# Seven block products in place of eight for 15 of 22 gate and up pairs of each feed-forward stage

## The chip, the cores and the metric

The kernel runs on one core of a Trainium2 chip. The metric is the time of one execution on the device in microseconds (us), as the median of several runs. The profile comes from one execution more, which a hardware profiler recorded.

The engines are TensorE (PE in the profile, with its weight loads apart as PEld), VectorE (DVE), ScalarE (ACT), GpSimd (POOL) and SyncE (SP). SBUF is the memory on the chip, PSUM the accumulators that TensorE writes; a PSUM tile here is one bank, 128 partitions by 512 numbers of 32 bits.

## The reference

Two layers of an encoder over 512 tokens of width 1024, all in float32. Each layer has three stages: feed-forward 1, a mixer (three kinds of attention, gates, a projection), feed-forward 2. Only the feed-forward stages change:

```python
def swiglu(x, w_gu, w_down):
    gate, up = jnp.split(x @ w_gu, 2, axis=-1)
    return (jax.nn.silu(gate) * up) @ w_down
...
y = swiglu(rmsnorm(h, ffn1_pre_g[l]), ffn1_w_gu[l], ffn1_w_down[l])
h = h + 0.5 * rmsnorm(y, ffn1_post_g[l])
```

Here `w_gu` is 1024 x 5632 (2816 gate columns, then 2816 up columns) and `w_down` 2816 x 1024. `rmsnorm` divides each token by the root of the mean of its squares plus 1e-6 and multiplies by a gain.

## The kernel before

**Layout.** Activations lie transposed: a tile is 128 of the 1024 channels on the partitions by 512 tokens. `h` is eight such tiles (KD = 8). The weights come as blocks of 128 x 128 in the order in which the program uses them (the list `order`), eight blocks (512 KB) to a DMA, `wr`, of which three buffers exist.

**Three products for one.** Every number is taken apart into a rounded part hi (type fp32r) and the rest lo, and a block product is three matmuls, hi x hi, hi x lo, lo x hi (`mm3`, L235 to L237), all summed in PSUM. The weights are taken apart on the fly by `ensure`: for each half of a `wr` tile, four blocks or 128 x 512, one ACT copy makes `wh` (L193) and one DVE subtraction makes `wl` (L194). `wblk` (L198) calls `ensure` two half tiles ahead of the use and issues the fetches, on the ACT queue. There are four buffers each of `wh` and `wl`.

**A feed-forward stage** (`ffn`, L413). The operand X is `h` times the gain of the pre-norm, in hi and lo; it is not divided by the root yet, since that scale (`rB`, one number for each token, the same on all partitions) is known only when the squares are summed. `begin` (L314) does the first three block columns in two halves of 256 tokens, as the stage before it ends. Then for each of KF = 22 pairs m a gate column block and an up column block are formed, 8 x 3 matmuls of 512 columns each, into PSUM tiles tagged mm and at. `finish` (L423) takes a pair: DVE gate times rB (L425), ACT Silu (L426), DVE times up (L427), then the split into hi and lo (L258 on ACT, L259 on DVE); up is not scaled by rB, which the norm behind the down projection takes out (its small constant is corrected by `e2`). Then `end` (L338) does the down projection, seven of eight row blocks whole, the last in two halves (`part`), while `refresh` updates `h` and makes the next operand.

**What sets the order.** The program is written in one stream; a scheduler places each engine's instructions from it, and buffers and semaphores do the rest. TensorE's stream of a pair is 24 matmuls into mm, then 24 into at. A tile of a pool that is used again waits until its last reader is done; a wait on a PSUM tile is for the whole tile.

Of the kernel before, what the change touches and what calls it, by code (L numbers as in the profile page):

```python
# [32 lines left out]
PAD = {"f": 168, "m": 168}  # L33
# [77 lines left out]
def encoder_kernel(ctx: ExitStack, tc: tile.TileContext, order, xT, wts, cols, rows, rpb, consts, tables, out):  # L111
# [9 lines left out]
    BUFS = {"h": 8, "x": 24, "t": 6, "r": 2, "wr": 3, "wh": 4, "wl": 4}  # L121
    ABUFS = {"f": {"a": 2 * KF}, "m": {"rr": 3, "tx": 5, "st": 16, "g": 10, "s": 2, "pt": 4}}
# [33 lines left out]
    rowt = cp.tile([P, L, ROWW], F32, tag="rowt", name="rowt")  # L156
    ones = cp.tile([P, P], F32, tag="ones", name="ones")
    half = cp.tile([P, NCOLS], F32, tag="half", name="half")
    misc = cp.tile([P, 2 * L + 1], F32, tag="misc", name="misc")
# [12 lines left out]
    stream = {"raw": [], "ready": [], "made": 0, "held": {}, "limit": 0}  # L172
# [9 lines left out]
    def ensure(n):  # L182
        while stream["made"] < min(n, NTILES * 2):
# [4 lines left out]
            if i in stream["held"]:  # L188
                tag = stream["held"][i]
                hi, lo = (big(tag, F32R, (P, HB, P), name="w") for _ in range(2))  # L190
            else:
                hi, lo = (sb.tile([P, HB, P], F32R, tag=t, name=nm(t), bufs=BUFS[t]) for t in ("wh", "wl"))
# [39 lines left out]
    V.tensor_scalar(out=half, in0=colt, scalar1=0.5, scalar2=None, op0=ALU.mult)  # L232

# [41 lines left out]
    def inv_rms(squares, n, nt, extra=None):  # L275
# [4 lines left out]
        if extra is None:  # L280
            V.tensor_scalar(out=ms[:, :nt], in0=tot[:, :nt], scalar1=1.0 / n, scalar2=EPS, op0=ALU.mult, op1=ALU.add)
        else:
            V.scalar_tensor_tensor(
                out=ms[:, :nt], in0=tot[:, :nt], scalar=1.0 / n, in1=extra, op0=ALU.mult, op1=ALU.add
            )
        A.activation(r[:, :nt], ms[:, :nt], AF.Sqrt)
        V.reciprocal(out=r[:, :nt], in_=r[:, :nt])
        rep = spread(r, nt)
        return rep, ms
# [24 lines left out]
    def begin(refresh, X, first, spare):  # L314
# [5 lines left out]
        stream["held"] = {i: spare for i in range(at + BUFS["wh"], stream["limit"])}  # L320
# [8 lines left out]
    def finish_rms(s):  # L329
        rB = big("r", name="rB")  # L330
        rep, ms = inv_rms(s.acc, D, NT)
        V.tensor_copy(rB, rep)
        return rB, rep, ms

    def fresh():
        return [(big("x", F32R, name="hi"), big("x", F32R, name="lo")) for _ in range(KD)]

    def end(name, l, X, group, tail, gcol, e2, after, hold=()):  # L338

        y = [big("x", name="y") for _ in range(KD)]  # L340
# [6 lines left out]
        if hold:  # L347
            at = len(order) + (KD - tail) * len(X)
            assert at % HB == 0 and len(hold) * HB == tail * len(X)
            stream["held"] = {at // HB + i: tag for i, tag in enumerate(hold)}  # L350
# [9 lines left out]
        def scales(i):  # L360
            hs = HALVES[i]
            extra = e2[:, 2 * i : 2 * i + 2] if e2 is not None else None
            return inv_rms(s.acc[:, hs], D, 2, extra)[0]
# [48 lines left out]

    def ffn(l, which, refresh, X):  # L413
        gu, dn = f"ffn{which}_w_gu", f"ffn{which}_w_down"
        firsts = [(gu, l, 0, 0), (gu, l, 0, KF), (gu, l, 0, 1)]
        (g0, u0, g1), s = begin(refresh, X, firsts, "a")
        u1 = dense1(gu, l, KF + 1, X, tag="at")
        rB, _, ms = finish_rms(s)
        e2 = small("e2", NT, 2)
        V.tensor_scalar(out=e2, in0=ms, scalar1=EPS, scalar2=None, op0=ALU.mult)  # L420
        act = []

        def finish(pg, pu):  # L423
            t = big("t", name="t")
            V.tensor_tensor(out=t, in0=pg, in1=rB, op=ALU.mult)  # L425
            A.activation(t, t, AF.Silu)  # L426
            V.tensor_tensor(out=t, in0=t, in1=pu, op=ALU.mult)  # L427
            act.append(split(t, "a"))

        finish(g0, u0)  # L430
        finish(g1, u1)
# [341 lines left out]
    for l in range(L):  # L773
        with open_phase("f"):
            refresh, X = ffn(l, 1, refresh, X)
        if l == 0:
            prepare()
# [62 lines left out]
```

## Time and profile before

| | |
|---|---|
| median of 3 runs | 2534.66 us (2534.31 to 2537.56) |
| the profiled execution | 2534.24 us, of which the span of the profile is 2532.5 |
| granted TensorE clock | 0.998 of full speed |
| matmuls | 12274 |
| read from HBM | 231.16 MB, 94 GB/s over the span |

The span is from the first to the last recorded instruction. In a row of a group of instructions come the line, the engine, the operation, the tile written and the tiles read (buffer numbers left out), the shape, the count, then the busy time, the mean of one in ns, and behind the second bar the idle time of the engine just before them with what ended most of it. A matmul's recorded duration is longer than its share of the stream, since matmuls overlap in the array: what one costs is the distance from its start to the next start.

### The profile page before, as it was taken

The page shows a single profiled execution, that of the slowest core. Times are in us where ns is not written, and L with a number is a line of the kernel's source. Part 1 is how long each engine was busy: PE and PEld are TensorE (multiplying, and loading weights), DVE is VectorE, ACT ScalarE, POOL GpSimd, SP SyncE. Part 2 cuts the span into 40 slices and gives each one's busy share as a digit, 9 for nine tenths or more (in the row PEclk, how much of TensorE's full clock was granted, in tenths as well). Part 3 has the DMA queues.
Part 4 walks back from the last instruction along what each step waited for, and adds up shares of the span by engine and source line. Part 5 has one row for each costly group of instructions (what it writes and reads, how often), then busy time and mean ns, then how long its engine had stood idle before and what let it go on. Part 6 is the DMA issues. An engine that isn't in the chain of part 4 may idle for free.

```text
span 2532.5 us, 32765 instructions
## 1 busy us (share of the span) xinstructions
PE 2506.4 (99%) x12274; PEld 2103.0 (83%) x12274; DVE 1380.1 (54%) x2687; ACT 1116.3 (44%) x2163; POOL 215.6 (9%) x197
## 2 busy tenths in 40 slices
PE   9999999999999999999999999999999999999998
PEld 8888888888778888888888888888887788888887
DVE  5444248867776464442364442488687764644423
ACT  5333245646555453333343332456465554533322
POOL 0000011001111220000110000200001112100002
PEclk9999999999999999999999999999999999999999
DMA  4232237435443322222232223374344423232222
GB/s 157 94 100 94 98 99 218 119 109 138 114 125 99 108 76 93 99 100 92 92 100 100 92 100 100 112 211 113 108 131 130 116 95 105 75 100 95 97 100 83
DMA packets 97375, 277.87 MB, mean 110 GB/s; under 512 B 13504, under 2 KB 17984, under 8 KB 97216
## 3 DMA queue, kind: packets, MB, share of 16 engines
q10 hardware_dynamic: 59616, 216.63, 25.9%
q1 hardware_dynamic: 37600, 59.15, 9.2%
q8 instruction: 96, 1.57, 0.3%
q14 instruction: 63, 0.52, 0.1%
HBM read 231.16 MB, written 6.29 MB: 94 GB/s over the span
## 4 chain that ended last, share of the span: by engine, by line
PE 91%; DVE 3%; issue 2%; DMA 1%; ACT 1%; POOL 1%; SPq 1%; POOLq 0%; DVEq 0%; ACTq 0%
PE mm L237 19%; PE mm L236 19%; PE mm L235 19%; PE at L236 9%; PE at L235 9%; PE at L237 9%; PE at L512 1%; POOL h L392 1%; PE o L515 1%; PE o L516 1%; PE at L484 1%; DMA sh<-raw 1%; PE at L269 1%; PE at L631 1%; PE at L485 1%
## 5 line engine op out<-in xcount | busy, mean ns | idle before, releaser
L193 ACT ACTIVATE wh<-wr 128x512 fp32r<-128x512 f32 x812 | 511.3, 631 | 1005.7 <-PE at L236 506.6
L194 DVE TENSOR_TENSOR wl<-wr,wh 128x512 fp32r<-128x512 f32 x812 | 582.7, 719 | 651.3 <-ACT wh L193 642.7
L237 PE MATMUL mm<-hi,wl 128*128 128x512 f32 (+1 forms) x2372 | 899.0, 379 | 4.8 <-DVE wl L194 4.4
L235 PE MATMUL mm<-hi,wh 128*128 128x512 f32 (+1 forms) x2372 | 897.1, 378 | 1.3 <-ACT wh L193 1.1
L236 PE MATMUL mm<-lo,wh 128*128 128x512 f32 (+1 forms) x2372 | 896.7, 378 | 0.1
L237 PEld LDWEIGHTS mm<-hi,wl 128*128 128x128 f32 x2372 | 447.2, 189 | 83.3 <-DVE wl L194 7.9
L235 PEld LDWEIGHTS mm<-hi,wh 128*128 128x128 f32 x2372 | 447.2, 189 | 77.8 <-ACT wh L193 1.3
L236 PEld LDWEIGHTS mm<-lo,wh 128*128 128x128 f32 x2372 | 447.3, 189 | 76.4 <-DVE lo L310 0.3
L235 PE MATMUL at<-hi,wh 128*128 128x512 f32 (+1 forms) x1028 | 394.3, 384 | 0.0
L236 PE MATMUL at<-lo,wh 128*128 128x512 f32 (+1 forms) x1028 | 393.8, 383 | 0.0
L237 PE MATMUL at<-hi,wl 128*128 128x512 f32 (+1 forms) x1028 | 393.6, 383 | 0.0
L235 PEld LDWEIGHTS at<-hi,wh 128*128 128x128 f32 x1028 | 193.5, 188 | 37.8
L237 PEld LDWEIGHTS at<-hi,wl 128*128 128x128 f32 x1028 | 193.5, 188 | 37.7
L236 PEld LDWEIGHTS at<-lo,wh 128*128 128x128 f32 x1028 | 193.4, 188 | 37.5
L304 POOL TENSOR_TENSOR ss<-ss,sq 128x512 f32<-128x512 f32 (+1 forms) x38 | 46.9, 1233 | 1391.3 <-ACT sq L303 1390.2
L427 DVE TENSOR_TENSOR t<-t,at 128x512 f32<-128x512 f32 x88 | 60.1, 687 | 127.4 <-PE at L237 124.2
L425 DVE TENSOR_TENSOR t<-mm,rB 128x512 f32<-128x512 f32 x88 | 60.5, 691 | 121.5 <-PE mm L237 121.3
L258 ACT ACTIVATE hi<-at 128x256 fp32r<-128x256 f32 (+2 forms) x168 | 75.8, 472 | 69.3 <-PE at L512 31.0
L259 DVE TENSOR_TENSOR lo<-at,hi 128x256 fp32r<-128x256 f32 (+2 forms) x168 | 87.1, 533 | 18.0 <-ACT hi L258 16.6
L392 POOL TENSOR_TENSOR h<-h,y 128x256 f32<-128x256 f32 x92 | 77.0, 867 | 83.2 <-DVE y L390 83.2
L530 POOL TENSOR_TENSOR sh<-sh,sinR 128x512 f32<-128x512 f32 x26 | 34.3, 1319 | 545.1 <-DMA sh<-raw 329.6
L497 ACT ACTIVATE s<-s,nmx 128x256 f32<-128x256 f32 (+1 forms) x128 | 70.4, 552 | 14.0 <-DVE nmx L488 7.5
(146 smaller groups left out, 2145.0 us busy)
## 6 DMA issues: line engine op xcount, KB each, us to landing
wr<-in_wts_dram ACTq DMA_DIRECT2D x413, 512.0 KB, 3.2
st<-hi SPq DMA_DIRECT2D x84, 128.0 KB, 2.3
st<-lo SPq DMA_DIRECT2D x84, 128.0 KB, 2.3
sh<-raw SPq DMA_DIRECT2D x104, 64.0 KB, 2.0
sw<-lo SPq DMA_DIRECT2D x36, 128.0 KB, 3.5
sw<-hi SPq DMA_DIRECT2D x36, 128.0 KB, 3.0
braw<-in_rpb_dram SPq DMA_DIRECT2D x16, 256.0 KB
kept<-h SPq DMA_DIRECT2D x16, 256.0 KB, 2.0
```

The costliest lines, as they stand in the source:

```text
L193: A.activation(hi, raw, AF.Copy)
L194: V.tensor_tensor(out=lo, in0=raw, in1=f(hi), op=ALU.subtract)
L235: PE.matmul(acc, w[0], x[0], start=start, stop=False)
L236: PE.matmul(acc, w[0], x[1], start=False, stop=False)
L237: PE.matmul(acc, w[1], x[0], start=False, stop=stop)
L258: A.activation(hi, src, AF.Copy)
L259: V.tensor_tensor(out=lo, in0=src, in1=f(hi), op=ALU.subtract)
L304: eng.tensor_tensor(out=self.acc[:, cs], in0=self.acc[:, cs], in1=sq[:, cs], op=ALU.add)
L392: adder.tensor_tensor(out=h[b][:, hs], in0=h[b][:, hs], in1=y[b][:, hs], op=ALU.add)
L425: V.tensor_tensor(out=t, in0=pg, in1=rB, op=ALU.mult)
L427: V.tensor_tensor(out=t, in0=t, in1=pu, op=ALU.mult)
L497: A.activation(ss[i], ss[i], AF.Exp, scale=-scale, bias=nmx[:, i : i + 1], accum_out=l[:, i : i + 1])
```

## The change

**Which products.** For the last 15 pairs of a stage (`PLAIN = 7` stay as they were) gate and up are no longer two separate columns of products. The pair's weights are a 2 x 2 matrix of blocks (gate, up by the first and second half of the 1024 channels) and the activation is a 2 x 2 matrix too (halves of channels by halves of tokens). Their product, eight block products in the plain way, is formed by seven, after Strassen and Winograd: `p1` to `p7`. Each is four blocks deep (HK = 4), three matmuls for each block, over 256 tokens: 84 matmuls of 256 columns for a pair (L648), where 48 of 512 stood. The operands of the products are sums and differences of the parts.

**Activation.** Since the sums of channels mix numbers of different tokens' halves, the activation is normalised first: `normal` multiplies by gain and rB (DVE, eight times). `less` makes the four differences t1 to t4, `divide` the hi and lo parts of the four parts and the differences. All that is put in a list, `stream["later"]`, of which each new weight half tile of the plain pairs runs one piece (`wblk`).

**Weights of a group.** A group is a pair done in this way. Its two `wr` tiles are fetched by the SP queue (`fetches`). DVE makes the sums `sum13` (128 x 1024), `sum2`, `sum4` (128 x 512) and the lo parts `low1`, `low13`, `low24` (128 x 1024) and `low12` (128 x 512); ACT makes the hi parts `high1`, `high13`, `high24` (128 x 1024) and `high12`.

**Accumulators.** A group has one PSUM tile mm with two halves, a and c, and half of one of two PSUM tiles at, b, which two matmuls a stage open (`seeds`). p1 goes into a; `seed` copies a to b on ACT (L688); p7 goes into c; `copy7` copies c to SBUF (L692); p6 adds to a; `copy2` copies a to SBUF (L695); p4 adds to c; `add21` on DVE adds c to that copy (L699); p2 adds to b, p5 to a; `add22` adds a (L703); p3 adds to a. At the end b and a hold the gate of the two token halves (`silu0`, `silu1`), and the SBUF tile v holds up with the sign turned; `gated` multiplies (L715).

**Behind it.** The result `act` stays in float32 and is taken apart late, by `cut` (L730, L731), during the last group and the down projection (three pieces to a weight half tile, `pace`). The sign goes into the post gain (`nhalf`, -0.5), and `e2` goes, as gate and up are both scaled now. Buffers: the 24 single x tiles become 12 pairs, `wh` and `wl` (4 each) four pairs `wp`. `prepare`, some small work on the lambdas and sinks, moves into the first feed-forward stage.

The core of the diff:

```diff
-    BUFS = {"h": 8, "x": 24, "t": 6, "r": 2, "wr": 3, "wh": 4, "wl": 4}
+    BUFS = {"h": 8, "x": 12, "t": 6, "wr": 3, "wp": 4}
...
+            for _ in range(min(stream["pace"], len(stream["later"]))):
+                stream["later"].pop(0)()
             stream["tile"] = stream["ready"].pop(0)
...
-        def finish(pg, pu):
-            t = big("t", name="t")
+        def finish(m, pg, pu):
+            t, v = big("t", name="t"), big("t", name="v")
             V.tensor_tensor(out=t, in0=pg, in1=rB, op=ALU.mult)
             A.activation(t, t, AF.Silu)
-            V.tensor_tensor(out=t, in0=t, in1=pu, op=ALU.mult)
-            act.append(split(t, "a"))
+            V.scalar_tensor_tensor(out=v, in0=pu, scalar=-1.0, in1=rB, op0=ALU.mult, op1=ALU.mult)
...
+            V.tensor_tensor(out=act[m], in0=t, in1=v, op=ALU.mult)
...
-        for m in range(2, KF):
-            finish(dense1(gu, l, m, X), dense1(gu, l, KF + m, X, tag="at"))
...
+        for m in range(2, PLAIN):
+            finish(m, dense1(gu, l, m, X), dense1(gu, l, KF + m, X, tag="at"))
...
+        def product(acc, w, x, start, stop):
+            for k in range(HK):
+                ws, xs = (w[0][:, k, :], w[1][:, k, :]), (hi[x][:, k, :], lo[x][:, k, :])
+                for n, (i, j) in enumerate(((0, 0), (0, 1), (1, 0))):
+                    PE.matmul(
+                        acc, ws[i], xs[j], start=start and k == n == 0, stop=stop and k == HK - 1 and n == 2,
+                        skip_group_check=True,
+                    )
...
+        def seed(g):
+            A.activation(groups[g]["b"], groups[g]["a"], AF.Copy)
...
+        for g in range(count):
+            more, last = g + 1 < count, g + 1 == count
+            p1(g)
+            if g:
+                add22(g - 1)
+            low24(g)
+            if more:
+                high1(g + 1)
+            seed(g)
+            if more:
+                sum13(g + 1)
+            p7(g)
+            if more:
+                high13(g + 1)
+                low1(g + 1)
+            copy7(g)
...
+            if g:
+                p3(g - 1)
+            if more:
+                sum2(g + 1)
+            if g:
+                silu1(g - 1)
+            if more:
+                high12(g + 1)
+            if g:
+                gated(g - 1)
+            p6(g)
+            if more:
+                low13(g + 1)
...
+            copy2(g)
+            p4(g)
+            add21(g)
...
+            p2(g)
+            silu0(g)
+            if more:
+                low12(g + 1)
+                sum4(g + 1)
+                fetches(g + 2)
+                p5(g)
+                high24(g + 1)
```

**TensorE, where one group's p7 begins.** The scheduler interleaves two groups. Here mm_1239 is the PSUM tile of the new group, mm_1120 that of the group before it; h_520 belongs to the last matmuls of p1, h_878 to p3 of the group before, ht_601 to p7. `[waits ...]` names the engine that is waited for.

```order
L648 MATMUL mm_1239<-h_520,h_1136 128x256
L648 MATMUL mm_1239<-l_521,h_1136 128x256
L648 MATMUL mm_1239<-h_520,l_1155 128x256
L648 MATMUL mm_1120<-h_878,h_1118 128x256 [waits DVE_49]
L648 MATMUL mm_1120<-l_879,h_1118 128x256
L648 MATMUL mm_1120<-h_878,l_1134 128x256
L648 MATMUL mm_1120<-h_878,h_1118 128x256
L648 MATMUL mm_1239<-ht_601,h_1153 128x256 [waits Activation_49]
L648 MATMUL mm_1239<-lt_602,h_1153 128x256
```

Four matmuls of p3 stand between p1's last and p7's first, which waits for the copy `seed` on ACT; p3 itself waits for `add22` on DVE. Over the whole group TensorE goes p1 (one matmul), p5 of the group before (12), p1 (11), p3 (4), p7 (12), p3 (8), p6 (12), p2 (4), p4 (12), p2 (8). In the kernel before the stream of a pair waits for weight parts alone, as where the next gate block begins:

```order
L236 MATMUL at_1282<-lo_134,wh_1266 128x512
L237 MATMUL at_1282<-hi_133,wl_1267 128x512
L235 MATMUL mm_1325<-hi_119,wh_1285 128x512 [waits Activation_49]
L236 MATMUL mm_1325<-lo_120,wh_1285 128x512
L237 MATMUL mm_1325<-hi_119,wl_1286 128x512 [waits DVE_49]
```

**DVE, one pair before and one group now.** Before, wl is a weight's lo part, the others belong to `finish`:

```order
L194 TENSOR_TENSOR wl_1598<-wr_1595,wh_1597 128x512
L425 TENSOR_TENSOR t_1629<-mm_1559,rB_432 128x512
L194 TENSOR_TENSOR wl_1614<-wr_1595,wh_1613 128x512
L194 TENSOR_TENSOR wl_1641<-wr_1638,wh_1640 128x512
L427 TENSOR_TENSOR t_1629<-t_1629,at_1594 128x512
L194 TENSOR_TENSOR wl_1657<-wr_1638,wh_1656 128x512
L259 TENSOR_TENSOR lo_1634<-t_1629,hi_1633 128x512
```

Now, from `add21` of one group to `sum13` for three groups later (add21, sum2, low12, sum4, add22, low1, low13, low24, gated, sum13):

```order
L699 TENSOR_TENSOR v_1394<-mm_1357,v_1394 128x256
L560 TENSOR_TENSOR wr_1459<-r_1494,wr_1457 128x512
L567 TENSOR_TENSOR w_1528<-wr_1459,w_1528 128x512
L570 TENSOR_TENSOR wr_1459<-wr_1459 128x512
L703 TENSOR_TENSOR v_1394<-mm_1357,v_1394 128x256
L549 TENSOR_TENSOR l_1510<-wr_1457,h_1491 128x1024
L557 TENSOR_TENSOR l_1543<-r_1494,h_1508 128x1024
L578 TENSOR_TENSOR l_1607<-wr_1459,h_1591 128x1024
L715 TENSOR_TENSOR a_1175<-t_1453,v_1394 128x512
L541 TENSOR_TENSOR r_1612<-wr_1577,wr_1575 128x1024
```

Seven operations of 512 have become ten, four of them twice as wide. `low24`, `gated` and `sum13` stand ahead of the next `add21`, for which p5 waits on TensorE.

**ACT, one group now.** In this order stand copy7, high24, silu1, copy2, high12, high1, high13, silu0 and the seed of the next group:

```order
L692 ACTIVATE v_1276<-mm_1239 128x256
L574 ACTIVATE h_1355<-wr_1223 128x1024
L710 ACTIVATE t_1217<-mm_1120 128x256
L695 ACTIVATE v_1276<-mm_1239 128x256
L564 ACTIVATE w_1410<-wr_1341 128x512
L545 ACTIVATE h_1373<-wr_1339 128x1024
L553 ACTIVATE h_1390<-r_1376 128x1024
L707 ACTIVATE t_1335<-at_896 128x256
L688 ACTIVATE at_895<-mm_1357 128x256
```

Before, the ACT row of a pair was four weight parts (L193), two fetches, a Silu and a hi part, all 512 wide; the two fetches now stand on SP.

More of the change, by code (lines that the diff above doesn't have):

```diff
@@ L32 @@
 WARM = 9
-PAD = {"f": 168, "m": 168}
+PLAIN = 7
+PAD = {"f": 184, "m": 184}
 SECOND = 1
@@ L436, in ffn @@
+        assert not stream["later"]
+        stream["pace"] = 1
         align()
```

353 lines of the change are left out of this document (295 added, 58 removed).

## The prediction

> **What bounds the kernel now.** I read the busy shares first, then the chain of work that ended last, then the costliest groups with the idle time before them.
>
> ```profile
> PE 2506.4 (99%) x12274; PEld 2103.0 (83%) x12274; DVE 1380.1 (54%) x2687; ACT 1116.3 (44%) x2163; POOL 215.6 (9%) x197
> ...
> PE 91%; DVE 3%; issue 2%; DMA 1%; ACT 1%; POOL 1%; SPq 1%; POOLq 0%; DVEq 0%; ACTq 0%
> ...
> L193 ACT ACTIVATE wh<-wr 128x512 fp32r<-128x512 f32 x812 | 511.3, 631 | 1005.7 <-PE at L236 506.6
> L194 DVE TENSOR_TENSOR wl<-wr,wh 128x512 fp32r<-128x512 f32 x812 | 582.7, 719 | 651.3 <-ACT wh L193 642.7
> L237 PE MATMUL mm<-hi,wl 128*128 128x512 f32 (+1 forms) x2372 | 899.0, 379 | 4.8 <-DVE wl L194 4.4
> ```
>
> TensorE (PE) works without a gap, and the others wait for it: ScalarE (ACT) stood still 1005.7 us ahead of the weight conversions, mostly because TensorE still read the buffers, while TensorE lost 4.8 us at L237. So a time is won only in TensorE's stream, and DVE and ACT have room. In one gate and up pair of the first stage this window (columns: TensorE, weight loads, DVE, ACT, POOL, clock) shows how much:
>
> ```profile
> 100.00:110.88 10.88, 10.88 (x49) 9.01 (x48) 4.66 (x8) 3.79 (x6) 0.00 (x0) 1.00 0.28 96
> ```
>
> The stretch that changes is 15 of 22 such pairs in four stages, 60 groups. The clock is 1.00.
>
> **What a matmul costs.** The timeline's rows give a start, a duration, the engine and the line. A pair is 48 matmuls of 512 columns, from the first row to the second; in the down projection's last part, 26 steps of 256 columns, in one accumulator, lie between the third and the fourth.
>
> ```profile
> 54.23 0.39 PE L235 MATMUL mm<-hi,wh 128*128 128x512 f32 x1
> ...
> 65.11 0.39 PE L235 MATMUL mm<-hi,wh 128*128 128x512 f32 x1
> ```
>
> ```profile
> 368.77 0.28 PE L235 MATMUL mm<-hi,wh 128*128 128x256 f32 x1
> ...
> 371.89 0.28 PE L237 MATMUL mm<-hi,wl 128*128 128x256 f32 x1
> ```
>
> That is 10.88/48 = 0.2267 us, and 3.12/26 = 0.120 us. A half as wide matmul costs 53%, not 50%. A Strassen group has 7 products x 4 blocks x 3 = 84 of them: 84 x 0.120 = 10.08 us. **The removal is thus at most 0.80 us a group, 48 us in all**, although an eighth of the arithmetic goes (1.36 us).
>
> [...]
>
> **What the new order adds on TensorE.** A product's accumulators a and c are halves of one PSUM tile, and waits go by the tile. So three reads stop the products that follow them: seed (a to b) ahead of p7, copy7 (c) ahead of p6, copy2 (a) ahead of p4. Their price comes from how fast ACT follows a last matmul and how TensorE restarts:
>
> ```profile
> 362.58 0.28 PE L237 MATMUL mm<-hi,wl 128*128 128x256 f32 x1
> ...
> 362.96 0.38 ACT L303 ACTIVATE sq<-mm 128x256 f32<-128x256 f32 x1 [4.00 <-PE mm L237]
> ...
> 363.24 0.47 ACT L345 ACTIVATE y<-mm,half 128x256 f32<-128x256 f32 x1
> ```
>
> ```profile
> 102.96 0.39 PE L237 MATMUL mm<-hi,wl 128*128 128x512 f32 x1
> ...
> 103.38 0.69 DVE L425 TENSOR_TENSOR t<-mm,rB 128x512 f32<-128x512 f32 x1 [1.59 <-PE mm L237]
> ...
> 103.99 0.68 DVE L194 TENSOR_TENSOR wl<-wr,wh 128x512 fp32r<-128x512 f32 x1
> ```
>
> ```profile
> 548.04 0.76 ACT L258 ACTIVATE hi<-at 128x256 fp32r<-128x256 f32 x2
> ...
> 548.46 0.19 PEld L515 LDWEIGHTS o<-hi,v 128*128 128x128 f32 x1 [0.20 <-ACT hi L258]
> 548.47 0.39 PE L515 MATMUL o<-hi,v 128*128 128x256 f32 x1
> ...
> 548.69 0.39 PE L237 MATMUL mm<-hi,wl 128*128 128x512 f32 x1
> ```
>
> From the last matmul's start to the reader it is 0.38 us; by the 512-column row 0.42, less 0.107 more columns, 0.32. The copy itself is the 0.38 us of 128x256; the load follows 0.04 after its end (548.04 + 0.38 = 548.42). Together 0.74 to 0.80 us. Behind p1 and ahead of p7 stand four matmuls of p3: p7 would start 5 x 0.12 = 0.60 after p1's last, so it is 0.14 to 0.20 late; and the first 256 columns after a stop take 0.22 (548.47 to 548.69) in place of 0.12. That is 0.24 to 0.30 us. copy2 has four matmuls of p2 as cover, the same sum. copy7 has eight of p3 (1.08 us): nothing; with four it would cost 0.27 too. I take **2 x 0.27**, so T = 10.08 + 0.54 = 10.62 us a group. Behind each waiting product stand all later ones on TensorE, so the loss is whole. Ends: 0 for both (if the waits end earlier than the rows say) and 2 x 0.35.
>
> **What DVE and ACT have to do in that time.** No operation of the trace is 1024 wide. The rows by form:
>
> ```profile
> L259 DVE TENSOR_TENSOR lo<-t,hi 128x512 fp32r<-128x512 f32 x88 | 60.9, 692 | 7.6
> ...
> L259 DVE TENSOR_TENSOR lo<-at,hi 128x384 fp32r<-128x384 f32 x64 | 34.4, 551 | 1.3 <-ACT hi L258 0.8
> ...
> L259 DVE TENSOR_TENSOR lo<-at,hi 128x256 fp32r<-128x256 f32 x64 | 26.9, 420 | 8.4 <-ACT hi L258 7.6 <-PE o L516 0.4
> ...
> L646 DVE SCALAR_TENSOR_TENSOR s<-s,lc,e 128x512 f32<-128x512 f32 x32 | 24.5, 767 | 0.1
> ```
>
> ```profile
> L258 ACT ACTIVATE hi<-t 128x512 fp32r<-128x512 f32 x88 | 55.3, 631 | 25.2 <-DVE t L427 25.2
> ...
> L303 ACT ACTIVATE sq<-h 128x256 f32<-128x256 f32 x84 | 29.8, 405 | 4.0 <-DVE ss L304 3.5
> ```
>
> DVE: 0.420 and 0.692 lie 0.272 apart per 256, so 1024 is 0.692 + 0.544 = 1.23; bounds 0.69 (one 512) and 1.38 (two). ACT: 0.631 + 2 x 0.226 = 1.08; bounds 0.63 and 1.26. I take the lines' values, nearest to three rows that lie on them. A group has on DVE four of 1024 (sum13, low1, low13, low24), four of 512, two of 256: 4.9 + 2.8 + 0.8 = 8.5 us of 10.62; back to back an operation starts 0.08 before the one ahead ends (103.38 + 0.69 against 103.99), about 7.7. ACT has three of 1024, one of 512, five of 256: 3.2 + 0.6 + 1.9 = 5.8.
>
> So nothing is full, but there is one **loop**. Count from the start of p7's last matmul. high24 needs its buffer back from p3's second-last matmul: 7 x 0.12 + 0.32 = 1.16. It ends at 2.23; low24 starts 2.27, gated 1.15 later (3.42), sum13 0.61 later (4.03), add21 1.15 later (5.18), and ends at 5.60; the load of p5 may go at 5.64. TensorE comes to that load after 8 + 12 + 4 + 12 + 8 + 1 = 45 matmuls and one stop: 5.40 + 0.27 = 5.67. **It fits by 0.03 us.** By the bounds below it only fits better; with 1.26 and 1.38 add21 would be later by 0.18 + 2 x 0.23 = 0.64. add22 has 9 matmuls of p1 as cover and 0.3 us to spare.
>
> The weights come by SP's queue in place of ACT's, which frees ACT of two issues a group.
>
> ```profile
> 104.71 0.34 ACTq L179 DMA_DIRECT2D wr<-in_wts_dram  x1
> ```
>
> ```profile
> wr<-in_wts_dram ACTq DMA_DIRECT2D x413, 512.0 KB, 3.2
> ...
> tab<-in_tables_dram SPq DMA_DIRECT2D x4, 256.0 KB, 5.1
> ```
>
> The second tile of a group gets its buffer when low1 of the group before ends, about 9.1 on the same count; sum13 needs it at 14.6 (10.62 + 4.03). Of 5.5 us an issue of 0.34 and a landing of 3.2 leave 2 us; with the slowest median of SP's, 5.1, it still just fits. SP has nothing else in these stages. Cost: nothing.
>
> Ahead of the groups, eight normalising operations (8 x 0.77), seven lo parts (7 x 0.69), four differences (4 x 0.73) and the first sums (2 x 1.23) are 16.4 us more on DVE within five plain pairs (54.4 us), which hold 5 x 4.66 = 23: covered, as 40 of 54 us. Were the cover gone, each late tile would stop TensorE by its own 0.69. The parts of act (hi and lo) move to the down projection, with nothing but the weight tiles beside them: covered there. The two matmuls that open the seed banks cost 2 x 0.2267 = 0.45 a stage. At a stage's first group low1 comes late by about one 512 operation (0.7), and the last two groups have cuts ahead of their copies, 0.2 as an estimate: **1.35 a stage, 5.4 us**; ends 2 and 12. The joints with the mixer and the mixer keep their order: nothing.
>
> **Sum.** 60 x (10.88 - 10.62) = 15.6, less 5.4, is 10.2 us. The profiled execution took 2534.24 us (span 2532.5), 0.4 below the median of 2534.66, so 2524.0 on its scale and **2524.5** against the median.
>
> **Rivals.**
> - *The stops vanish* (the reads end before TensorE comes back, sooner than the rows say): T = 10.08, 48 - 5.4 = 42.6, **2492 us**; with one stop gone, 2508. For it: 548.46 shows how soon a load follows. Against it: 0.38 + 0.38 stands in rows, four matmuls don't cover it. Chance 0.12.
> - *The loop of high24, low24, gated, sum13, add21 becomes the bound.* This ends **slower**. If the 1024-wide operations cost two 512s (1.26, 1.38), p5 waits 0.64 - 0.03 = 0.61 and restarts for 0.10: T = 11.33, 60 x 0.45 + 5.4 = 32 more, **2567 us**. It decides from T = 10.79, where the gain no longer pays the 5.4: a lateness of 0.07 behind a restart of 0.10, or 3% on those five operations. For it: only 0.03 us spare, five operations in series. Against: three widths on one line. Chance 0.20.
> - *DVE doesn't overlap its operations here.* Then three starts are 0.08 later each: 0.24 - 0.03 + 0.10 = 0.31, T = 10.93, 60 x 0.05 + 5.4 = 8 more, **2543 us**. The rows at 103.38 and 103.99 speak against it; that operations waiting for others overlap as well isn't shown. Chance 0.08. [...]
> - *Fetches land late* (over 5.1 us): each group late by what exceeds it, at 6 us some 0.9, T = 11.5, **2577 us**. For it: 1 MB must come in 10.6 us, as before. Chance 0.04.
>
> **How the numbers follow.** The forecast, T from 10.45 to 10.75, has 0.56: 60 x 0.43 - 5.4 = 20 to 60 x 0.13 - 5.4 = 2.4 us gained, 2514 to 2532. The range reaches to one stop gone (2508) and, on the other side, past no overlap (2543) to **2546**; outside lie the rest of the first, most of the second and the fourth. A change of 0.2% (5 us) is about what a measurement can tell. Faster than 2529.6 are 0.47 of the forecast's and all of the first rival's chance, 0.59; within 0.2% the other 0.09 and 0.11 of the slower ones that only just decide, 0.20; slower 0.21.
>
> **What would show it.** Steps of the p products 0.120 us apart; p7 and p4 with idle time behind ACT of some 0.2 us in each group; p5 with none behind DVE; a group's pitch 10.6. high and low operations of 1024 at 1.08 and 1.23. I am wrong if p5 waits for add21 in each group (the loop), if p7 doesn't wait (first rival), if sum13 waits for a DMA, or if the mixer or the plain pairs change their length.

## The result, and the profile after

The changed kernel took **2548.32 us** (median, 2547.10 to 2552.22) beside 2534.48 us (2533.36 to 2537.56) of the kernel before in the same session: a ratio of 1.0055 [1.0038, 1.0073], 13.8 us slower. I had forecast 10.2 us faster, and the time lies 2.3 us above the range.

First the page of the kernel after: busy time of each engine, the shares of the chain that ended last, and the groups that bear on the forecast (busy us, mean ns, then the idle time just before and what ended it).

```profile
PE 2501.6 (98%) x14442; PEld 2181.9 (86%) x14442; DVE 1692.7 (66%) x3030; ACT 1261.5 (50%) x2431; POOL 216.6 (9%) x197
...
PE 85%; DVE 5%; DMA 3%; issue 2%; POOL 2%; ACT 1%; SPq 1%; POOLq 0%; ACTq 0%; DVEq 0%
...
L246 PE MATMUL mm<-X,w 128*128 128x512 f32 (+1 forms) x1128 | 431.8, 383 | 8.3 <-ACT w L201 6.4
L248 PE MATMUL mm<-X,w 128*128 128x512 f32 (+1 forms) x1128 | 429.6, 382 | 3.8 <-DVE w L202 3.8
...
L648 PE MATMUL mm<-ht,h 128*128 128x256 f32 x960 | 284.1, 296 | 1.0 <-DVE v L699 0.2
...
L648 PEld LDWEIGHTS mm<-ht,h 128*128 128x128 f32 x960 | 183.0, 191 | 23.5 <-ACT v L695 10.4
...
L578 DVE TENSOR_TENSOR l<-wr,h 128x1024 fp32r<-128x1024 f32 x60 | 73.4, 1224 | 117.7 <-ACT h L574 117.7
```

TensorE's busy time fell by 4.8 us, yet the span grew by 14.2 (2532.5 to 2546.7): TensorE now waits. The chain says the same: TensorE's share of it went from 91% to 85%, while DVE went from 3 to 5, DMA from 1 to 3 and POOL from 1 to 2. The rows at L648 belong to the groups; `mm<-ht,h` holds a part of p7, p6, p4 and p5. Its loads stand idle for 23.5 us over 60 groups, 10.4 of it for copy2 ahead of p4 (L695) and 9.3 for seed ahead of p7 (L688), as forecast; add21 ahead of p5 (L699) stops them for 1.8. L246 and L248 are outside the groups.

To see where the time went I cut each profile at the matmuls that sum the squares of a norm. A stage's *body* reaches from the sums of its pre norm to the first sum of its post norm (for the first token half), its *tail* from there to the second sum (for the second half). The two sums of the first stage's post norm, before and after:

```profile
363.92 0.61 PE L278 MATMUL o<-ones,ss 128*128 128x1 f32 x4
...
377.44 0.58 PE L278 MATMUL o<-ones,ss 128*128 128x1 f32 x4 [0.24 <-DVE ss L304]
```

```profile
360.73 0.61 PE L289 MATMUL o<-ones,ss 128*128 128x1 f32 x4
```

The second sum of the kernel after starts at 375.60. So the first sum came 3.2 us earlier (363.92 to 360.73), but the tail grew from 13.51 to 14.87. With all stages and the two mixers cut in this way ("rest" is what lies between the pieces and at the ends), the differences to the kernel before are, in us:

| | four stage bodies | stage tails | two mixer bodies | mixer tails | rest | span |
|---|---|---|---|---|---|---|
| before, absolute | 1333.3 | 49.9 | 981.1 | 17.2 | 151.0 | 2532.5 |
| after | -12.3 | +6.2 | +15.3 | +6.8 | -1.7 | +14.2 |

The groups brought 12.3 us, and 26.5 us (14.2 + 12.3) went where the diff writes no operation anew: into the tails, and into the mixers.

**The groups, as forecast.** The timeline of one steady group in the kernel after (start, duration, engine, line; x is how many instructions a row joins):

```profile
204.87 0.37 ACT L688 ACTIVATE at<-mm 128x256 f32<-128x256 f32 x1 [1.74 <-PE mm L648]
...
215.44 0.37 ACT L688 ACTIVATE at<-mm 128x256 f32<-128x256 f32 x1 [1.68 <-PE mm L648]
```

```profile
204.97 0.28 PE L648 MATMUL mm<-h,h 128*128 128x256 f32 x1
205.29 0.39 PE L648 MATMUL mm<-ht,h 128*128 128x256 f32 x1
205.51 0.28 PE L648 MATMUL mm<-lt,h 128*128 128x256 f32 x1
...
205.29 0.19 PEld L648 LDWEIGHTS mm<-ht,h 128*128 128x128 f32 x1 [0.24 <-ACT at L688]
```

From seed to seed it is 10.57 us here; steady groups take 10.57 and 10.63 in turn, 10.60 in the mean (forecast 10.62). p7's first load waits 0.24 us for seed (204.87 + 0.37 = 205.24); the steps around it are 0.32 and 0.22 us in place of 0.12 each, so the stop costs 0.30, and copy2's costs 0.26 by the same steps.

**The tail.** Here POOL adds y to the residual h, ACT makes the hi part X of the next stage's operand from it and DVE the lo part; TensorE is in the last quarter of the down projection, whose weights ACT and DVE split. POOL of the kernel before, then of the kernel after:

```profile
366.79 6.88 POOL L392 TENSOR_TENSOR h<-h,y 128x256 f32<-128x256 f32 x8 [9.54 <-DVE y L390]
```

```profile
363.72 3.46 POOL L413 TENSOR_TENSOR h<-h,y 128x256 f32<-128x256 f32 x4 [9.43 <-DVE y L411]
368.67 3.43 POOL L413 TENSOR_TENSOR h<-h,y 128x256 f32<-128x256 f32 x4 [1.49 <-DVE y L411]
```

Eight additions without a gap became four, a gap of 1.49 us, and four. DVE shows why; first before, then after:

```profile
366.30 1.41 DVE L390 TENSOR_TENSOR y<-y,at 128x256 f32<-128x256 f32 x4
367.72 1.06 DVE L194 TENSOR_TENSOR wl<-wr,wh 128x512 fp32r<-128x512 f32 x1
368.70 0.96 DVE L310 SCALAR_TENSOR_TENSOR lo<-h,colt,hi 128x256 fp32r<-128x256 f32 x1
369.59 0.74 DVE L390 TENSOR_TENSOR y<-y,at 128x256 f32<-128x256 f32 x2
370.25 0.99 DVE L310 SCALAR_TENSOR_TENSOR lo<-h,colt,hi 128x256 fp32r<-128x256 f32 x1
371.17 0.74 DVE L390 TENSOR_TENSOR y<-y,at 128x256 f32<-128x256 f32 x2
```

```profile
363.23 1.40 DVE L411 TENSOR_TENSOR y<-y,at 128x256 f32<-128x256 f32 x4
364.63 1.08 DVE L202 TENSOR_TENSOR w<-wr,w 128x512 fp32r<-128x512 f32 x1
365.63 2.62 DVE L315 SCALAR_TENSOR_TENSOR X<-h,colt,X 128x256 fp32r<-128x256 f32 x4
368.18 1.40 DVE L411 TENSOR_TENSOR y<-y,at 128x256 f32<-128x256 f32 x4
369.50 1.14 DVE L202 TENSOR_TENSOR w<-wr,w 128x512 fp32r<-128x512 f32 x1
370.56 2.60 DVE L315 SCALAR_TENSOR_TENSOR X<-h,colt,X 128x256 fp32r<-128x256 f32 x4
```

Before, one lo part stands between the y products, two of which follow at once; now four lo parts (L315) stand there in a row, and each waits for its hi part, and that for POOL's addition (2.62 us for four, while one of these operations takes 0.47 at the least). So the next four y start 2.55 us after the weight part ahead of the L315 (365.63 to 368.18), POOL stands idle, and the weight parts behind the L315 are late for TensorE. Its waits before, then after:

```profile
373.14 0.39 PE L237 MATMUL mm<-hi,wl 128*128 128x256 f32 x1 [0.73 <-DVE wl L194]
...
374.62 0.39 PE L237 MATMUL mm<-hi,wl 128*128 128x256 f32 x1 [0.15 <-DVE wl L194]
```

```profile
370.69 0.50 PE L248 MATMUL mm<-X,w 128*128 128x256 f32 x2 [1.25 <-DVE w L202]
...
373.21 0.39 PE L246 MATMUL mm<-X,w 128*128 128x256 f32 x1 [1.66 <-ACT w L201]
```

That is 2.91 us of waits for weight parts in this tail, where it was 0.88.

**The mixer.** At the first mixer's entry the order on DVE changed too. Of the operations on the bias tables (`bedge`, `bmid`) nine now stand ahead of the norm's `ms`, where eight stood, and one of them waits for its table's transfer, with the norm behind it. DVE before, then after, then TensorE after:

```profile
399.05 0.55 DVE L567 TENSOR_TENSOR bmid<-braw,mask 128x384 f32<-128x384 f32 x1
399.52 0.75 DVE L567 TENSOR_TENSOR bedge<-braw,mask 128x256 f32<-128x256 f32 x2
400.36 0.16 DVE L281 TENSOR_SCALAR ms<-o 128x4 f32<-128x4 f32 x1
```

```profile
399.27 0.42 DVE L939 TENSOR_TENSOR bedge<-braw,mask 128x256 f32<-128x256 f32 x1 [4.05 <-DMA braw<-in_rpb_dram]
...
400.55 0.55 DVE L939 TENSOR_TENSOR bmid<-braw,mask 128x384 f32<-128x384 f32 x1
401.02 0.15 DVE L291 TENSOR_SCALAR ms<-o 128x4 f32<-128x4 f32 x1
```

```profile
401.92 1.51 PE L280 MATMUL at<-cons,rs 128*128 128x128 f32 x8 [3.10 <-DVE rs L293]
...
404.08 0.63 PE L246 MATMUL mm<-X,w 128*128 128x512 f32 x1
404.51 0.63 PE L247 MATMUL mm<-X,w 128*128 128x512 f32 x1
```

`ms` starts 4.89 us after the norm's sums (396.13), where it was 0.98 (399.38). The order alone doesn't set this loss: `x_pairs` below has the same nine ahead, and its `ms` comes 0.98 after the sums in the first mixer and 2.14 in the second.

TensorE's last two rows lie 0.43 us apart where 0.2267 is usual. Windows of this stretch (window, length, busy us of TensorE, weight loads, DVE, ACT and POOL, then granted clock, DMA share, GB/s) say why: the clock.

```profile
399.00:402.60 3.60, 0.68 (x6) 0.68 (x7) 2.88 (x8) 0.20 (x1) 0.00 (x0) 1.00 0.29 109
402.60:406.00 3.40, 3.40 (x12) 2.82 (x11) 1.85 (x4) 1.00 (x2) 1.76 (x2) 0.50 0.54 161
406.00:409.40 3.40, 3.40 (x16) 2.76 (x16) 2.48 (x4) 1.52 (x4) 0.88 (x1) 1.00 0.21 50
```

So this late joint was paid twice: by the 3.10 us of waiting for rs and by the 3.4 us at clock 0.50 behind it. In the kernel after there are 23.9 us at clock 0.50 in five places ahead of the program's end, in the kernel before 3.4 in one. Half of the 20.5 us between them, 10 us, is an estimate of its worth, and part of the 26.5 us.

### The profile page after: what moved, and what is told of

Same layout as the page of the kernel before. It is cut to its first block, busy times and chain, and to the rows that moved or that the text cites. A ratio compares the mean times of both kernels' runs of the same rounds, so it can differ in the third digit from the quotient of the medians.

```text
span 2546.7 us, 37855 instructions
## 1 busy us (share of the span) xinstructions
PE 2501.6 (98%) x14442; PEld 2181.9 (86%) x14442; DVE 1692.7 (66%) x3030; ACT 1261.5 (50%) x2431; POOL 216.6 (9%) x197
## 3 DMA queue, kind: packets, MB, share of 16 engines
q1 hardware_dynamic: 54880, 122.07, 16.9%
## 4 chain that ended last, share of the span: by engine, by line
PE 85%; DVE 5%; DMA 3%; issue 2%; POOL 2%; ACT 1%; SPq 1%; POOLq 0%; ACTq 0%; DVEq 0%
PE mm L648 21%; PE mm L248 13%; PE mm L246 13%; PE mm L247 13%; PE at L248 4%; PE at L246 4%; PE at L247 4%; PE at L648 3%; DMA sh<-raw 1%; PE at L883 1%; POOL h L413 1%; PE o L887 1%; PE at L855 1%; PE o L886 1%; DVE X L315 1%
## 5 line engine op out<-in xcount | busy, mean ns | idle before, releaser
L202 DVE TENSOR_TENSOR w<-wr,w 128x512 fp32r<-128x512 f32 x584 | 419.7, 724 | 408.6 <-ACT w L201 405.8
L201 ACT ACTIVATE w<-wr 128x512 fp32r<-128x512 f32 x584 | 364.0, 629 | 579.3 <-PE mm L248 267.9
L246 PE MATMUL mm<-X,w 128*128 128x512 f32 (+1 forms) x1128 | 431.8, 383 | 8.3 <-ACT w L201 6.4
L248 PE MATMUL mm<-X,w 128*128 128x512 f32 (+1 forms) x1128 | 429.6, 382 | 3.8 <-DVE w L202 3.8
L247 PE MATMUL mm<-X,w 128*128 128x512 f32 (+1 forms) x1128 | 430.0, 381 | 0.9 <-DVE X L315 0.7
L648 PE MATMUL mm<-ht,h 128*128 128x256 f32 x960 | 284.1, 296 | 1.0 <-DVE v L699 0.2
L648 PE MATMUL mm<-lt,h 128*128 128x256 f32 x960 | 271.1, 282 | 0.0
L648 PE MATMUL mm<-ht,l 128*128 128x256 f32 x960 | 270.8, 283 | 0.0
L246 PEld LDWEIGHTS mm<-X,w 128*128 128x128 f32 x1128 | 214.8, 190 | 43.4 <-ACT w L201 7.6
L248 PEld LDWEIGHTS mm<-X,w 128*128 128x128 f32 x1128 | 214.3, 190 | 39.3 <-DVE w L202 4.8
L247 PEld LDWEIGHTS mm<-X,w 128*128 128x128 f32 x1128 | 214.8, 190 | 35.6 <-DVE X L315 1.3
L648 PEld LDWEIGHTS mm<-ht,h 128*128 128x128 f32 x960 | 183.0, 191 | 23.5 <-ACT v L695 10.4
L648 PEld LDWEIGHTS mm<-lt,h 128*128 128x128 f32 x960 | 183.5, 191 | 0.0
L648 PEld LDWEIGHTS mm<-ht,l 128*128 128x128 f32 x960 | 183.1, 191 | 0.0
L578 DVE TENSOR_TENSOR l<-wr,h 128x1024 fp32r<-128x1024 f32 x60 | 73.4, 1224 | 117.7 <-ACT h L574 117.7
L648 PE MATMUL mm<-h,l 128*128 128x256 f32 x480 | 136.2, 284 | 2.3 <-DVE l L549 2.3
L648 PE MATMUL mm<-h,h 128*128 128x256 f32 x480 | 136.1, 284 | 0.0
L648 PE MATMUL mm<-l,h 128*128 128x256 f32 x480 | 135.6, 283 | 0.0
```

Of the source, the lines that this page charges most:

```text
L201: A.activation(hi, raw, AF.Copy)
L202: V.tensor_tensor(out=lo, in0=raw, in1=f(hi), op=ALU.subtract)
L246: PE.matmul(acc, w[0], x[0], start=start, stop=False)
L247: PE.matmul(acc, w[0], x[1], start=False, stop=False)
L248: PE.matmul(acc, w[1], x[0], start=False, stop=stop)
L578: V.tensor_tensor(out=W[g]["l24"], in0=raws[g][1], in1=f(W[g]["h24"]), op=ALU.subtract)
```

## The experiments

**Theory:** the loss comes from keeping hi and lo (and gate tiles and y) in pairs of one tile, of which the order of DVE and ACT at the joints (where one stage ends and the next begins) is a consequence. **Rivals:** the weight pairs wp do it; or the work that Strassen's products add on DVE and ACT runs into the joints. All times are medians of timed rounds; the kernel before took 2535.5 to 2536.1 us on the chip beside them, and ratios are to it.

### One part of the change alone, in the kernel before

`x_pairs`: the kernel before, with its x tiles in twelve pairs and nothing of Strassen.

```diff
-    BUFS = {"h": 8, "x": 24, "t": 6, "r": 2, "wr": 3, "wh": 4, "wl": 4}
+    BUFS = {"h": 8, "x": 12, "t": 6, "r": 2, "wr": 3, "wh": 4, "wl": 4}
...
+    def pair(name, dt=F32R):
+        return sb.tile([P, 2, T], dt, tag="x", name=nm(name), bufs=BUFS["x"])
...
-        return [(big("x", F32R, name="hi"), big("x", F32R, name="lo")) for _ in range(KD)]
+        both = [pair("X") for _ in range(KD)]
+        return [(t[:, 0, :], t[:, 1, :]) for t in both]
...
-        y = [big("x", name="y") for _ in range(KD)]
+        ys = singles("y")
+        y = [ys(b) for b in range(KD)]
```

> The kernel before, with only one piece of the change: the x buffers as 12 pairs in place of 24 singles, so that the hi and the lo part of an operand X share one tile, and so do two blocks of y and of the first gates. No Strassen product, no other part. In the changed kernel the four feed-forward stages gained 12.3 us inside (3.4, 2.8, 3.1, 3.0 between their two norms) and all the rest lost 26.6. Theory A (the pairs change the order that the scheduler gives DVE and ACT where a stage ends and in the mixers): 2555 to 2562 us, some 20 to 27 above before, with the half-speed stretches of the TensorE clock (5 more in the changed kernel) there too. Rival B (what is lost comes from the groups: DVE, the queue of SP, cuts of act in the down projection): 2535, the same as before.

Measured: 2551.62 us, 1.0061 [1.0046, 1.0076]. **15.5 us slower without one Strassen product.** Its POOL rows in the first tail have the gap of the changed kernel:

```profile
367.83 3.47 POOL L408 TENSOR_TENSOR h<-h,y 128x256 f32<-128x256 f32 x4 [9.53 <-DVE y L406]
372.79 3.42 POOL L408 TENSOR_TENSOR h<-h,y 128x256 f32<-128x256 f32 x4 [1.48 <-DVE y L406]
```

`w_pairs`: the kernel before, with each weight's hi and lo parts in one tile.

```diff
-                hi, lo = (sb.tile([P, HB, P], F32R, tag=t, name=nm(t), bufs=BUFS[t]) for t in ("wh", "wl"))
+                hi, lo = wpart("w")
```

> The kernel before with only the weights' hi and lo parts in one tile (wp, 4 pairs) in place of wh and wl, 4 each. A buffer then comes free for the hi part one matmul later. Theory A: the same as before within 3 us, since the order of DVE at the joints stays as it was. Rival C (the weight buffers cause the waits on DVE w L202 and ACT w L201 that the changed kernel shows at its joints, 1.4 and 1.8 us each): 10 us or more above before.

Measured: 2540.5 us, 1.0021 [1.0011, 1.0031], 4.4 us slower; the stage tails hardly move (+0.4), the mixer bodies do (+6.5). DVE's order in the tails is that of before, as expected, but inside the mixers it isn't.

`xw_pairs`: both edits.

> The kernel before with both: x as 12 pairs and the weights' parts in wp. By the two runs apart, 15.5 + 4.4 = 20 us above before if they add: 2552 to 2560. What lies between this and the changed kernel (2548) is then the worth of the seven products themselves with all that belongs to them: 12 us gained inside the stages by the trace, so 2560 would close the sum and 2553 would leave 7 us of another loss. If the two overlap (the same waits counted twice), 2551.

Measured: 2556.33 us, 1.0077 [1.0062, 1.0092], 20.8 us slower: 15.5 and 4.4 add up within the interval.

### Which of the pairs

`y_pairs`: as `x_pairs`, but the operands hi and lo are single tiles again; y and the gate tiles stay paired.

```diff
-    BUFS = {"h": 8, "x": 12, "t": 6, "r": 2, "wr": 3, "wh": 4, "wl": 4}
+    BUFS = {"h": 8, "x": 4, "X": 16, "t": 6, "r": 2, "wr": 3, "wh": 4, "wl": 4}
...
-        both = [pair("X") for _ in range(KD)]
-        return [(t[:, 0, :], t[:, 1, :]) for t in both]
+        return [(big("X", F32R, name="hi"), big("X", F32R, name="lo")) for _ in range(KD)]
```

> The kernel before with y and the first gates in pairs, but the hi and lo parts of X in tiles of their own (16). Theory A, made narrower: it is hi and lo of one operand in one tile that changes the order, so this one runs as before, 2533 to 2539; the printed order of DVE in the mixer is that of before. Rival: the pairs of y delay POOL's addition to h, 2545 or more.

Measured: 2535.8 us, 1.0002 [0.9992, 1.0012]. The pairs of y cost nothing; it is the operands' pairs.

`hi_lo_apart`: as `x_pairs`, but a pair holds the hi parts of two channel blocks, another their lo parts, so that no tile is both read and written by one split.

```diff
+        his, los = [], []
+        for _ in range(KD // 2):
+            his.append(pair("X"))
+            los.append(pair("X"))
+        return [(his[b // 2][:, b % 2, :], los[b // 2][:, b % 2, :]) for b in range(KD)]
```

> The kernel of x_pairs, with the pairs cut the other way: the hi parts of two blocks share a tile, and the lo parts of two blocks another. Theory A (hi and lo of one operand in one tile): most of the 15.5 us goes, 2536 to 2544. Rival (any tile shared by two makes the scheduler hold X together): 2551 again.

Measured: 2550.56 us, 1.0054 [1.0039, 1.0069]. That hi and lo *of one block* share a tile is thus not the reason: sharing with the neighbouring block's part does it as well. My explanation of the order fell here.

What order goes with which tiles can be read from DVE's rows in the first tail of every run (y is a y product, w a weight's lo part, x an operand's lo part):

| order | runs |
|---|---|
| y y y y w x y y x y y w x w x w x w x | before, `w_pairs`, `y_pairs`, and of the kernels below `s_all`, `s_x`, `s_banks`, `s_banks6` |
| y y y y w x x x x y y y y w x x x x w w w | after, `x_pairs`, `xw_pairs`, and below `banks` |
| y y y y w x x y x x y y y w x x w x x w w | `hi_lo_apart` |

The old order stands in every kernel whose operands are single tiles, and in none with operand pairs (the runs with priorities, next, have orders of their own); where the lo parts of two blocks share a tile, they come in twos.

### The order, by priorities

Could the weight parts be put ahead by hand? `after_wfirst` is the changed kernel with a higher priority (60 places) for the two operations that split a weight, `after_wyfirst` with one for these (1000) and for the y product and the addition behind it (200).

```diff
-            A.activation(hi, raw, AF.Copy)
-            V.tensor_tensor(out=lo, in0=raw, in1=f(hi), op=ALU.subtract)
+            with tc.high_priority(60):
+                A.activation(hi, raw, AF.Copy)
+                V.tensor_tensor(out=lo, in0=raw, in1=f(hi), op=ALU.subtract)
```

> The changed kernel, with the two operations that make a weight half tile (L201, L202) given 60 places of precedence in the scheduler. On DVE at a stage's end they then stand between the operations on X again, not behind four of them. Theory A: the waits of TensorE for w in the last part of the down projection (1.4 and 1.8 us) go, 2 to 3 us for each of three joints and what the half clock costs there: 2536 to 2543. Rival B: 2548, no change.

> As the last, with 1000 places for the weights and 200 for the scaling of y and its addition to h (L411, L413), so that the eight y stand ahead of the X. Theory A: like the last or better by what the chain from y over POOL's addition to X gains at the end of the mixer, 2530 to 2543. Rival B: 2548.

Measured: 2558.73 us, 1.0089 [1.0074, 1.0104], and 2557.65 us, 1.0084 [1.0069, 1.0099]: both worse than the change, which shows 1.0055, and both far from what was expected. In the second the stage tails lost only 2.9 us in place of 6.2, so putting y ahead does help there; but the mixer bodies went from +15.3 to +22.0, the bodies from -12.3 to -5.4. A priority moves operations at every place where it applies, and so these two don't tell what the tails alone would be worth.

### The pairs undone, in the changed kernel

`s_all`: the changed kernel with single tiles for everything; each 1024-wide operation of a group becomes two of 512.

```diff
-    BUFS = {"h": 8, "x": 12, "t": 6, "wr": 3, "wp": 4}
+    BUFS = {"h": 8, "x": 24, "t": 6, "wr": 3, "wh": 4, "wl": 4}
...
-            V.tensor_tensor(out=W[g]["l24"], in0=raws[g][1], in1=f(W[g]["h24"]), op=ALU.subtract)
+            for j in range(2):
+                V.tensor_tensor(out=W[g]["l24"][j], in0=raws[g][1][:, j], in1=f(W[g]["h24"][j]), op=ALU.subtract)
```

> The changed kernel with its x buffers as 24 singles and wh, wl apart, as the kernel before has them; the 128x1024 operations of a group become two of 128x512 each (DVE 14 in place of 10, ACT 12 in place of 9). The seven products stay. Theory A (the shared tiles cost what the change lost outside of the groups): the stages gain their 12 us as in the changed kernel, their tails and the mixers are as before: 2518 to 2527. In the loop the halves let low24 start after the first half of high24, so a group's pitch stays at 10.6; a rival says that four more operations on DVE (14 x about 0.6) make the pitch 10.8 or more: 2535. Rival B (the loss comes from the groups' traffic or from act's late split): 2548, as the changed kernel.

`s_x`: the same, but the weight pairs wp stay, and with them the 1024-wide `sum13`, which writes one.

> As the last, but the weights' hi and lo parts stay in one tile (wp). Theory A with the price of w_pairs alone (+4.4 us): 2523 to 2531, above the last one by 2 to 6.

Measured: `s_all` 2534.51 us, 0.9993 [0.9983, 1.0002]; `s_x` 2538.83 us, 1.0011 [1.0002, 1.0021]. On DVE the order of `s_all` in the mixers is that of the kernel before, operation for operation, and its tails are back at the old length. POOL in its first tail:

```profile
365.70 6.90 POOL L412 TENSOR_TENSOR h<-h,y 128x256 f32<-128x256 f32 x8 [9.54 <-DVE y L410]
```

Some 14 us come back with the pairs undone (16 by the ratios), 9.5 of them (11) with the x tiles alone; `s_x` less `s_all` is 4.3 us, which agrees with the 4.4 of `w_pairs`. The price is in the groups: their pitches are 10.59, 10.60 and 11.12 us, 10.77 in the mean of the three, and the bodies gain 5.3 us in place of 12.3, as the rival in the expectation said. There the loads wait 5.5 us for add21 ahead of p5, in 40 of the 60 groups, so the loop of the prediction's second rival shows once the wide operations are halved.

Its mixer bodies are still 4.5 us longer than before, in an order that is the same on DVE. The traces show a part of it: in the first mixer DVE waits 8.4 us for POOL's `sh` in place of 4.9, and POOL waits for the transfer `sh<-raw`. And they show more transfers that land later: the first mixer's weight fetches (x71 or x72 on ACT's queue) land 3.2 to 3.4 us after their issue, in the median, in each of the six kernels without the seven products, 3.6 to 3.8 in each of the eight with them. Why they land later, no run shows. A single profile isn't exact here either: `s_all`, `s_banks` and `s_banks6`, whose mixers are the same code, have 492.6, 491.8 and 496.7 us for the first mixer body.

### The stops in a group

The forecast held that p7 and p4 stop because a and c are halves of one PSUM tile. `banks` gives c a tile of its own; nothing else in the code of the changed kernel differs.

```diff
-            d["a"], d["c"] = acc[:, :HT], acc[:, HT:]
+            d["a"] = acc[:, :HT]
...
-            product(groups[g]["c"], wsel(g, "s3"), "t3", False, False)
+            groups[g]["c"] = bank("mm")[:, HT:]
+            product(groups[g]["c"], wsel(g, "s3"), "t3", True, False)
```

> The changed kernel with a and c of a group in two PSUM tiles (of the four mm) in place of halves of one, p7 opening its own. Then seed, copy7 and add21 no longer stand between a product and the next one into the other half: p7 waits for nothing, p6 for the seed, p4 for copy7, p5 for copy2, all covered. My term of 2 x 0.27 us a group for two stops goes: pitch 10.1 to 10.4 (DVE's loop may hold it above 10.08), 60 x 0.2 to 0.5 = 12 to 30 us less than the changed kernel: 2518 to 2536. If the stops cost nothing (they overlap something else that binds), 2548.

Measured: 2521.25 us, 0.9951 [0.9934, 0.9968]. The pitch is 10.02 to 10.14 us, 10.08 in the mean, just 84 x 0.120; the bodies gain 39.6 us, while tails and mixers lose as much as in the changed kernel (+5.4, +14.4, +6.8).

`s_banks` is `banks` and `s_all` together, `s_banks6` has 16 groups and six plain pairs (`PLAIN = 6`) besides.

> Both: singles and two PSUM tiles a group. Theory A and the term of the stops add up: 48 us from the products, less about 5 for start and end of a stage and what DVE's throughput takes: 2488 to 2503. If DVE (8.5 us and four operations more of 10.1) holds the pitch at 10.4: 2508.

> The kernel of s_banks with six plain pairs a stage in place of seven, so 16 groups: four pairs more at 10.08 in place of 10.88 is 3.2 us less, 2489 to 2494. If the 16.4 us of normalising and differences no longer fit beside four plain pairs on DVE, TensorE waits at the start of the groups: 2495 or more.

Measured: **2495.45 us, 0.9839 [0.9823, 0.9855]**, and 2492.27 us, 0.9827 [0.9813, 0.9842], the lowest median; the intervals of the two overlap. The page of `s_banks`: busy time, the chain, and the row that held the stops.

```profile
PE 2462.2 (99%) x14442; PEld 2169.1 (87%) x14442; DVE 1705.8 (68%) x3270; ACT 1277.4 (51%) x2611; POOL 215.7 (9%) x197
...
PE 88%; DVE 3%; DMA 3%; issue 2%; ACT 1%; POOL 1%; SPq 1%; POOLq 0%; DVEq 0%; ACTq 0%
...
L652 PE MATMUL mm<-ht,h 128*128 128x256 f32 x960 | 272.0, 283 | 0.0
```

TensorE is at 99% again, and the row with the matmuls that open p7, p6, p4 and p5 takes 283 ns in the mean, as the other rows of L652, where 296 stood: no stop is left.

The stage table for the runs, differences to the kernel before in us:

| | bodies | stage tails | mixer bodies | mixer tails | rest | span |
|---|---|---|---|---|---|---|
| `x_pairs` | 0 | +4.4 | +5.3 | +7.1 | -1.3 | +15.6 |
| `w_pairs` | 0 | +0.4 | +6.5 | 0 | -0.1 | +6.9 |
| `xw_pairs` | 0 | +7.8 | +8.6 | +6.8 | -2.5 | +20.8 |
| `y_pairs` | 0 | +0.1 | +0.4 | 0 | -0.6 | 0 |
| `hi_lo_apart` | 0 | +4.6 | +9.6 | +7.1 | -3.7 | +17.5 |
| `after_wfirst` | -11.0 | +6.4 | +23.9 | +10.5 | -6.2 | +23.6 |
| `after_wyfirst` | -5.4 | +2.9 | +22.0 | +11.3 | -6.0 | +24.7 |
| `s_all` | -5.3 | 0 | +4.5 | 0 | +1.0 | +0.3 |
| `s_x` | -5.8 | +0.3 | +12.4 | 0 | -1.7 | +5.2 |
| `banks` | -39.6 | +5.4 | +14.4 | +6.8 | -0.6 | -13.6 |
| `s_banks` | -45.7 | 0 | +5.0 | 0 | +2.1 | -38.7 |
| `s_banks6` | -49.3 | 0 | +8.1 | 0 | 0 | -41.2 |

The tails of both kinds follow the operands' pairs row by row: +11.5 to +16.9 in sum with them, +0.4 or less without. The mixer bodies are longer with either pair, but there the entries of single profiles differ by up to 3.6 us where the mixers' code is the same (+4.5, +5.0, +8.1), so small differences in that column say nothing.

## Why the prediction was wrong

- **A group's length, right.** T = 10.62 forecast, 10.60 in the mean. The two stops cost 0.26 and 0.30 us (0.27 each forecast), and copy7 none; `banks` takes them away and leaves 10.08, the figure worked out from 0.120 us a matmul.
- **The wide operations, right.** DVE at L578 1224 ns (1.23 forecast); ACT at L574 1059 ns (1.08), by this row of the kernel after:

```profile
L574 ACT ACTIVATE h<-wr 128x1024 fp32r<-128x1024 f32 x60 | 63.5, 1059 | 32.3 <-PE mm L648 21.0 <-DVE wr L570 10.7
```

- **The loop, right.** add21 was in time for p5 in the steady groups. The loads' 1.8 us behind it fall at the first and last groups of a stage. The price that the rival put on two 512s in place of a 1024 was too dear: `s_all`, which has them (and whose low24 may start sooner), shows 10.77 in place of 11.33.
- **Start and tail of a stage, 5.4 us: a little too dear.** The bodies gained 12.3 us; 60 x (10.88 - 10.60) = 16.8 less 12.3 leaves 4.5.
- **DVE overlaps its operations here, right:** L549 starts at 214.46 and L557, behind it, at 215.60, though the first lasts 1.21 us: an overlap of 0.07, where 0.08 was forecast.
- **Fetches, plain pairs and ends of the bodies at nothing: right** as far as the bodies' gain, 2.1 us better than forecast, shows it.
- **"The joints with the mixer and the mixer keep their order: nothing" — the step that failed.** It was worth 26.5 us. I had looked at the order inside the groups, where the diff writes new operations, and took the rest to be as before since its code is. But the order is made by a scheduler, and it depends on the tiles, as `x_pairs` shows; the line "the 24 single x tiles become 12 pairs" alters those in every stage and mixer. DVE's rows at the first tail, the lo parts by fours in place of ones, could have been compared without a run. None of my rivals looked there: they placed the slow side in the loop or the fetches, both inside the groups. Only the last sentence named the sign that came, a mixer that changes its length; it had no price and no chance.

How the 26.5 us divide: `xw_pairs` shows that both pairs make the kernel before 20.8 us slower by themselves. With the 12.3 us of the bodies this would leave 8.5 us slower, and 13.8 were measured: **some 5 us stay open.** By the stage table they lie in the mixer bodies (+15.3, where `xw_pairs` has +8.6). Candidates are the wait for the bias table (4.05 us on DVE) with its 3.4 us at clock 0.50, and the 4.5 us that `s_all` also loses in the mixers without any pair, where transfers land later; no run takes these apart. Open, too, is why the scheduler keeps the parts of paired operands together; `hi_lo_apart` only shows that it isn't the sharing of hi with its own lo. That the pairs cost the time is shown by the runs. That they cost it through the order is read from the traces: the tails keep their old order in each kernel with single operands and in none with operand pairs, and the waits of the tails stand behind the lo parts that were moved. The runs that changed the order alone, by priorities, moved too much to show it, and no run tested by itself whether a buffer shared by two comes free later.

## What to carry to other kernels

Where a scheduler sets the order, a change of buffers (two operands in one tile) can change the order at the joints that use them, as `x_pairs` did (15.5 us): compare the order of each engine at stage ends and starts, not only where code was written, and try the buffer edit alone in the old kernel. Two accumulators that are read at different times deserve a PSUM tile each: here that was worth 27.3 us (39.6 - 12.3), more than the change had hoped to gain. Fewer, wider operations saved 7 us in the groups here (12.3 - 5.3), and the tiles in pairs that they need cost 15.5 and 4.4 at the joints and in the mixers.

## What the runs showed of the hardware that was not expected

- **In four of five places the clock stood at half behind a window in which TensorE was busy for about half of the time.** In the kernel after, windows at clock 0.50, each 3.4 or 6.8 us long, stand in five places; the first is shown above. Two windows of the same view ahead of another of them (905) and in it (909):

```profile
904.30:907.70 3.40, 1.70 (x13) 1.44 (x13) 2.65 (x6) 2.68 (x7) 1.20 (x2) 1.00 0.00 0
```

```profile
907.60:911.00 3.40, 3.40 (x18) 3.40 (x18) 1.58 (x5) 2.14 (x8) 0.00 (x0) 0.52 0.18 19
```

TensorE was busy for 1.70 of 3.40 us, no single wait longer than 1.70, and the next 3.4 us came at 0.52; the windows ahead of the other three have 1.52, 1.73 and 1.74 us busy. But that share doesn't decide it alone. Another window of the kernel after, and the one behind it:

```profile
1887.40:1890.80 3.40, 1.63 (x8) 1.01 (x6) 1.05 (x4) 1.03 (x3) 1.27 (x1) 1.00 0.20 81
1890.80:1894.20 3.40, 3.15 (x16) 2.80 (x17) 3.19 (x11) 1.86 (x4) 0.00 (x0) 1.00 0.41 97
```

TensorE was busy for 1.63 us only, and the clock stayed at 1.00. What else enters, no run here shows.
- **Width saved little on DVE here.** The 240 more operations of `s_banks` against the kernel after (x3270 against x3030), with the wide ones halved, made DVE's busy time 13.1 us longer (1705.8 against 1692.7), 55 ns for each. Start to start a wide one takes 1.14 us in the kernel after (214.46 to 215.60), a narrow one 0.60 in `s_all` (L569 at 208.26, L562 at 208.86), so two narrow ones cost 0.06 more. With the stops gone the groups had room for them: the bodies of `s_banks` gained more than those of `banks`.
